# Written-out engine orders for the banded attention pairs, an earlier second norm and three sums on another engine, in a two-layer encoder trunk

## The chip, the cores and the metric

The kernel runs on one core of a Trainium2 chip. The core has five engines with their own instruction queues: TensorE (PE: matrix products and transposes through it), VectorE (DVE), ScalarE (ACT), GpSimd (POOL) and SyncE (SP), which issues the loads and stores. Each queue is worked off in its own order, and the engines wait for one another through semaphores. The metric is the device time of one launch in microseconds, as the median over several runs.

## The reference

The trunk has two layers on 1024 tokens of width 1024, all in fp32. Per layer: a modulated RMSNorm and one input projection, three groups of attention heads side by side, a group-wise RMSNorm, one output projection with a gated residual, then a second modulated RMSNorm and a SwiGLU feed-forward block (hidden width 2816).

```python
h = rms_norm(x, g_attn[l]) * (1 + sc_a) + sh_a
qa, ka, va, qb, kb, vb, qc, kc, vc = split_cols(h @ w_in[l], IN_SPLITS)
ya = neighborhood_attention(...)     # A, 4 heads: 8x16 window on a 16x64 grid, relative bias
yb = sliding_window_attention(...)   # B, 6 heads: |i-j| <= 128, T5 bias, a sink logit
yc = axial_attention(...)            # C, 6 heads: dense, rotary
y = concat([rms_norm(ya, ga), rms_norm(yb, gb), rms_norm(yc, gc)])
x = x + gt_a * (y @ w_o[l])
h = rms_norm(x, g_ffn[l]) * (1 + sc_f) + sh_f
gate, up = split_cols(h @ w_gu[l], (FFN_HIDDEN, FFN_HIDDEN))
x = x + gt_f * ((silu(gate) * up) @ w_down[l])
```

A and B are banded: a block of 128 queries sees at most three blocks of 128 keys. In the kernel the tokens of A are sorted by columns of the grid, so that its window has the same three-block band.

## The kernel before, in words

An fp32 product is formed from parts: each operand is split into a rounded part (`hi`, written by ScalarE) and the rest (`lo`, a subtraction, mostly on VectorE), and three products hi·hi, lo·hi, hi·lo are added in PSUM (`mm3`). So every operand costs a copy on ScalarE and a subtraction on VectorE.

The order of instructions on an engine is set by a scheduler, which orders by dependencies and its own estimate. Where the program calls `pin(engines, True)`, each instruction of these engines is chained behind the one before it in program order, so the written order is the engine's order. GpSimd is pinned throughout the attention; TensorE, ScalarE and VectorE are not in the kernel before.

**Attention.** One list `stream` has 64 pairs; a pair is two blocks of 128 queries of one head: pairs 0 to 23 are dense (C), 24 to 39 are A, 40 to 63 are B. The main loop runs over `n` and keeps several pairs in work: the transposes of pair n (`turn`), the products with V of pair n-1 (`pv`), and the scores of a pair further on (`qk`), three ahead for C, five ahead for the bands (`AHEAD`, `AHEAD_B`).

A band pair goes through these steps:

- scores (`sA`, `sB`): two products per block (rounded and low part of the keys), into one tile of `psS` (two buffers, each with a bank for either block).
- bias step: one VectorE instruction per block adds the bias `z`, writes `pr` and takes the row's extreme (CUSTOM_DVE_ANT in the trace), with an accumulator read.
- exponential: one ScalarE instruction per block with its sum, and an accumulator read.
- division: one reciprocal on VectorE, then two GpSimd multiplications (`pr<-pr,rs`).
- transposes (`T`): four of the inner blocks and one or two of the edge blocks, in tiles of `psT` (three buffers); ScalarE writes the rounded part (`pt<-T` CAST), VectorE the low part (`pt<-T`), and an `edge` copy goes to VectorE in even and ScalarE in odd pairs.
- products with V (`pv`), rounded and low part, into `psV`, which has a single bank shared by two neighbouring pairs; the result has its two halves on different partitions.
- `combine`, in odd pairs: ScalarE copies one half (`cmb<-pv`), VectorE adds both into `y`, and the bank is free again.

A head has four pairs; the first and the last see one edge block, the inner two see both. Beside this run the group norms: squares (`gsq`, `gss`) on ScalarE, sums on GpSimd, statistics on TensorE (`ps_st`) and a short chain of small VectorE steps (`isq`, `rstd`), the transposes `ps_r` with their copies `rb`, and the multiplications `y<-y,rb` on GpSimd. Near the end the first products of the output projection (`ps_o`) and the splits of `w_o` are mixed in.

**Gate/up.** The feed-forward products use a seven-product scheme on 2x2 blocks (`PRODUCTS`); quarter numbers `q` alternate gate (even) and up (odd). The first two products of the first seven quarters (`EARLY`) need only the first half of the tokens and run while the norm of the second half is still being made: `rstd_rows` yields once after the statistics and once with the row of reciprocal roots spread over the partitions (`ps_r`, by four transposes). Then `t2_part`, `t3_part` and `t4_part` make the operands t1, t2, t3, t4 and 22 on VectorE and ScalarE (`h_norm` is the VectorE step that reads `ps_r`). After that the other five products of quarter 0, then of quarter 1, and so on follow; `sg` and `u` hold their sums. Weight operands (`wpt`, from `ws` and `wr`) are made ahead by VectorE, ScalarE and, from the tenth on, GpSimd in turns.

Of the kernel before, what the change touches and what calls it, by code (L numbers as in the profile page):

```python
# [10 lines left out]
F32 = mybir.dt.float32  # L11
# [74 lines left out]
def trunk(ctx: ExitStack, tc, A, C, out):  # L86
# [732 lines left out]
    for l in range(2):  # L819
# [421 lines left out]
        class Pair:  # L1241
# [38 lines left out]
            def combine(self):  # L1280

                r0 = (self.row % 2) * 64
                o0 = 64 - r0
                half = self.p // 2
                t = atp.tile([P, H], F32, name="cmb", tag="cmb", bufs=1)
                act.copy(t[r0 : r0 + 64], self.pvt[o0 : o0 + 64])
                to = y[r0 : r0 + 64, self.row // 2, :]
                a, b = self.pvt[r0 : r0 + 64], t[r0 : r0 + 64]
# [26 lines left out]
        class PairC(Pair):  # L1315
# [21 lines left out]
            def pv(self, part):  # L1337
                self.products(
                    [
                        (kb * 4 + i, slice(0, 256), [t[:, i, :] for t in self.pt[kb]])  # L1340
                        for kb in range(2)
                        for i in range(4)
                    ],
                    part,
                )

# [37 lines left out]
        class Band(Pair):  # L1384
# [10 lines left out]
            def qk(self, c):  # L1395
                rs, p, sk = self.rs, self.p, self.sk
                if c == 0:
                    self.s = psS.tile([P, 2, 512], F32, name=self.name, tag="S")
                s, pr = self.s, self.pr
                j = 2 * p + c  # L1400
                a, b = self.spans[c]
                for i in range(2):
                    pe.matmul(
                        s[:, c, a:b], self.q[:, j * P : (j + 1) * P],
                        self.k[i][:, (j - 1) * P + a : (j - 1) * P + b],
                        start=(i == 0), stop=(i == 1),
                    )
                sv, pw, z = s[:, c, a:b], pr[:, c, a:b], self.bias(j, a, b)
                if z.ndim > 2:
                    sv, pw = (t.rearrange("p (b k) -> p b k", k=P) for t in (sv, pw))  # L1410
                dve.tensor_tensor_reduce(
                    out=pw, in0=sv, in1=z, scale=1.0, scalar=BIG if sk is None else sk,
                    op0=ALU.add, op1=ALU.min, accum_out=rs[:, c : c + 1],
                )
                e = pr[:, c, a : b + (sk is not None)]
                act.activation(
                    e, e, AF.Exp, bias=rs[:, c : c + 1], scale=-1.0,
                    accum_out=rs[:, 2 + c : 3 + c],
                )
                self.finish(pr[:, c, a:b])  # L1420

            def turn(self, c):
                pr = self.pr
                T = t_tile()
                if c == 0:
                    self.pt = [pt_tile() for _ in range(2)]
                    for b in range(2):
                        for i in range(2):
                            pe.transpose(
                                T[:, 2 * b + i, :], pr[:, b, (1 - b + i) * P : (2 - b + i) * P],  # L1430
                                ident,
                            )
                    hv, lv = (
                        t[:, 0:2, :].rearrange("p i (c q) -> p c i q", c=2) for t in self.pt
                    )
                    split_pt(T.rearrange("p (c i) q -> p c i q", c=2), hv, lv)
                    return
                e = self.e = atp.tile([P, 2, P], F32, name="edge", tag="edge", bufs=3)
                n = 0
                for left, here in ((True, self.left), (False, self.right)):  # L1440
                    if here:
                        src = pr[:, 0, 0:P] if left else pr[:, 1, 2 * P : 3 * P]
                        pe.transpose(T[:, n, :], src, ident)
                        n += 1
                if self.p % 2:
                    act.copy(e[:, 0:n], T[:, 0:n])
                else:
                    dve.tensor_copy(e[:, 0:n], T[:, 0:n])

            def pv(self, part):  # L1450
# [8 lines left out]
                self.products(movs, part)  # L1459
# [121 lines left out]
        AHEAD, AHEAD_B = 3, 5  # L1581
        pin((pool,), True)
        made, done = 0, len(first_pairs)
        for n in range(-AHEAD - 1, N + 1):
            ahead = AHEAD if n + AHEAD < 24 else AHEAD_B
            begin = range(done, min(n + ahead + 1, N))
            for i in range(2):
                if 0 <= n < N:
                    pairs[n].turn(i)
                while unfinished:  # L1590
                    unfinished.pop(0)()
                if 0 <= n - 1 < N:
                    pairs[n - 1].pv(i)
                for m in begin:
                    if m < made:
                        pairs[m].qk(i)
            done = max(done, min(begin.stop, made))
            while made < min(N, n + ahead + 2):
# [27 lines left out]
            m = n - 1  # L1626
            for end, (chunks, width) in norms.items():
                if begins[end] <= m <= end and (m - begins[end]) % 8 == 7:
# [22 lines left out]
        pin((pool,), False)  # L1651
# [195 lines left out]
        def gu_product(q, p, a):  # L1847
# [131 lines left out]
        for q in range(EARLY):  # L1979
            for i in range(2):  # L1980
                a = [w[:, 4 * i : 4 * i + 4] for w in early[q]]
                gu_product(q, PRODUCTS[i], a)
            if q + 4 < EARLY:
# [5 lines left out]
            if q == 1:  # L1989
                rows = next(norm)  # L1990
# [357 lines left out]
```

## Time and profile before

| | |
|---|---|
| runs, median (lowest to highest) | 2423.01 us (2418.51 to 2429.48), 3 runs |
| profiled execution | 2422.97 us, span 2421.1 us, mean granted clock 0.994 |
| TensorE busy | 2350.5 us, 97% of the span |
| VectorE, ScalarE, GpSimd busy | 1766.8, 1194.3, 753.4 us |
| bands, layer 0 and layer 1 | first add into `y` at 394.0 and 1574.8 us |
| start of gate/up in layer 0 | first product 583.4 us, remaining products of quarter 0 from 622.9 us |

A line of a group of instructions reads: line, engine, operation, output<-inputs, shape, count, then busy time and mean duration, then the idle time before it and what ended it. All engines' instructions are recorded in one helper, so their line is always L49; the names of the tiles tell them apart. A line of a stretch reads: window, its length, then for TensorE's products, TensorE's weight loads, VectorE, ScalarE and GpSimd the busy time with the count, then the granted clock, the DMA share and GB/s. A line in order of time reads: start, duration (of several in a row together), engine, operation, output<-inputs, shape, count, and in brackets the idle time before it with what ended it. Products overlap in the pipeline, so their durations are longer than the distance of their starts.

### The profile page before, as it was taken

Reading aid. Unit: us, or ns where it says so; the run is one execution under the profiler, and the core shown is the slowest. Engines: PE = TensorE matmul, PEld = TensorE weight load, DVE = VectorE, ACT = ScalarE, POOL = GpSimd, SP = SyncE. Lnnn points to the kernel's source line nnn. Section 1 sums busy time; section 2 is a strip of 40 time slices with the busy share of each in tenths; the row PEclk is TensorE's granted clock in tenths of the full one; section 3 lists DMA queues with packets and bytes.
Section 4 is the critical chain, followed back from the end, with each engine's and each line's share of the span. In section 5 each row is a group of like instructions: output and inputs, shape, how many; then the busy total and the mean of one; then the engine's idle time right before and its main releaser. Section 6 shows DMA issues by size and latency. Waiting matters only on the chain.

```text
span 2421.1 us, 33439 instructions
## 1 busy us (share of the span) xinstructions
PE 2350.5 (97%) x11733; PEld 1955.2 (81%) x11733; DVE 1766.8 (73%) x2782; ACT 1194.3 (49%) x2250; POOL 753.4 (31%) x725
## 2 busy tenths in 40 slices
PE   8999999999999999999999999999999999999998
PEld 5778798888787887888787879987878888888886
DVE  5756898976958888586677579988787545447865
ACT  3421788954543333344543148897454333334443
POOL 1530345610344344300036114464005444430001
PEclk9999999999999999999999999999999999999999
DMA  8478215154245454586434851142524332329643
GB/s 263 149 237 274 62 27 145 47 193 138 87 145 178 157 189 147 176 268 195 148 93 120 283 178 27 45 140 70 194 93 153 125 100 96 114 92 304 209 129 109
DMA packets 305335, 356.95 MB, mean 147 GB/s; under 512 B 51964, under 2 KB 221788, under 8 KB 305168
## 3 DMA queue, kind: packets, MB, share of 16 engines
q1 hardware_dynamic: 283296, 342.07, 44.4%
q10 hardware_dynamic: 21504, 12.59, 2.0%
q8 instruction: 92, 1.51, 0.2%
q14 instruction: 75, 0.61, 0.1%
q0 software_dynamic: 368, 0.17, 0.0%
HBM read 269.79 MB, written 88.63 MB: 148 GB/s over the span
## 4 chain that ended last, share of the span: by engine, by line
PE 48%; DVE 4%; issue 4%; DMA 2%; ACT 2%; POOL 2%; ACTq 0%; SPq 0%; POOLq 0%; DVEq 0%
PE ps_w L49 21%; PE ps_d L49 14%; PE ps_o L49 3%; PE pv L49 2%; PE T L49 2%; PE ps_v L49 2%; PE sC L49 2%; DMA qkd<-qko 1%; ACT pr L49 1%; PE ps_c L49 1%; POOL ct L49 1%; PE ps_ab L49 0%; DVE acc L49 0%; DMA graw<-gpd 0%; POOL pr L49 0%
## 5 line engine op out<-in xcount | busy, mean ns | idle before, releaser
L49 PE MATMUL ps_d<-wpt 128*128 128x512 f32 x1848 | 424.3, 390 | 2.4 <-ACT wpt L49 2.1
L49 PEld LDWEIGHTS ps_d<-wpt 128*128 128x128 f32 x1848 | 345.5, 188 | 76.4 <-issue 3.0
L49 POOL TENSOR_SCALAR pr<-pr,rs 128x1024 f32<-128x1024 f32 (+2 forms) x248 | 187.0, 768 | 227.8 <-DVE rs L49 212.8
L49 POOL TENSOR_TENSOR sg<-sg,u 128x512 f32<-128x512 f32 x86 | 125.5, 1461 | 354.5 <-ACT sg L49 117.9
L49 PE MATMUL pv<-pt,vs 128*128 128x256 f32 x1088 | 181.4, 297 | 7.3 <-ACT pt L49 2.7
L49 ACT CAST wpt<-w 128x512 fp32r<-128x512 f32 x154 | 95.7, 621 | 185.8 <-PE ps_d L49 168.0
L49 DVE TENSOR_TENSOR pt<-T,pt 128x512 fp32r<-128x512 f32 x272 | 178.5, 682 | 8.5 <-ACT pt L49 7.1
L49 PE MATMUL T<-identr,pr 128*128 128x128 f32 x1176 | 175.6, 273 | 2.6 <-ACT edge L49 0.8
L49 ACT CAST pt<-T 128x512 fp32r<-128x512 f32 x272 | 153.1, 586 | 40.5 <-PE T L49 38.1
L49 ACT COPY u<-ps_w 128x512 f32<-128x512 f32 x128 | 75.1, 586 | 192.1 <-PE ps_w L49 192.0
L49 DVE TENSOR_TENSOR wpt<-w,wpt 128x512 fp32r<-128x512 f32 x154 | 108.9, 707 | 82.1 <-ACT wpt L49 82.1
L49 POOL TENSOR_TENSOR wpt<-ws,wpt 128x512 fp32r<-128x512 f32 x80 | 111.6, 1395 | 180.8 <-ACT wpt L49 133.9
L49 PEld LDWEIGHTS pv<-pt,vs 128*128 128x128 f32 x1088 | 143.9, 189 | 21.1 <-DVE y L49 11.1
L49 PEld LDWEIGHTS T<-identr,pr 128*128 128x128 f32 x1176 | 139.9, 140 | 19.7 <-ACT edge L49 2.2
L49 DVE SCALAR_TENSOR_TENSOR acc<-wmt,condT,acc 128x512 f32<-128x512 f32 (+1 forms) x98 | 119.2, 1225 | 47.8 <-DMA wmt<-in_w_mod_dram 47.2
L49 ACT CAST wpt<-ws 128x512 fp32r<-128x512 f32 x176 | 107.8, 622 | 61.4 <-issue 26.6
L49 DVE TENSOR_TENSOR wpt<-ws,wpt 128x512 fp32r<-128x512 f32 x96 | 81.6, 861 | 60.3 <-ACT wpt L49 60.2
L49 DVE TENSOR_TENSOR wpt<-graw,wpt 128x512 fp32r<-128x512 f32 x154 | 110.0, 715 | 19.0 <-ACT wpt L49 19.0
L49 DVE TENSOR_REDUCE rs<-sC 128x1 f32<-128x1024 f32 x88 | 107.3, 1221 | 16.4 <-PE sC L49 12.4
L49 DVE TENSOR_TENSOR ws<-wr 128x512 f32<-128x512 f32 x88 | 80.0, 911 | 51.3 <-POOL wpt L49 48.1
L49 ACT CAST wpt<-graw 128x512 fp32r<-128x512 f32 x154 | 95.0, 617 | 43.3 <-DMA graw<-gpd 37.9
L49 PE MATMUL ps_w<-h22h,wpt 128*128 128x512 f32 x352 | 111.2, 397 | 4.6 <-ACT sg L49 3.6
(298 smaller groups left out, 5964.4 us busy)
## 6 DMA issues: line engine op xcount, KB each, us to landing
wr<-in_w_gu_dram SPq DMA_DIRECT2D x92, 512.0 KB, 4.1
gpd<-sg SPq DMA_DIRECT2D x154, 256.0 KB, 4.4
graw<-gpd SPq DMA_DIRECT2D x76, 512.0 KB, 3.6
w<-in_w_down_dram SPq DMA_DIRECT2D x110, 256.0 KB, 5.4
wmt<-in_w_mod_dram SPq DMA_DIRECT2D x48, 512.0 KB, 6.4
qk<-qkd SPq DMA_DIRECT2D x44, 512.0 KB, 6.8
wst<-in_w_o_dram SPq DMA_DIRECT2D x32, 512.0 KB, 3.7
wmt<-in_w_mod_dram SPq DMA_DIRECT2D x64, 256.0 KB, 3.8
```

Of the source, the lines that this page charges most:

```text
L49: ins = op(*args, **kwargs)
```

## The change

1. **Bands.** `Band.qk` is split into `scores` (four score products of both blocks, then both bias steps), `exps` and `divide`; `turn` does all transposes at once and leaves the low part for later (`low`); `pv` does both parts. `combine` is split: `fold` copies one half to `cmb`, `combine` adds. For n from 24 on, TensorE, ScalarE and VectorE are pinned, and the loop body writes out a step: low part of pair n-1, add of n-3, scores and bias steps of n+4, exponentials of n+3, transposes of n, products of n-2 with their fold, division of n+2. `AHEAD_B` goes from 5 to 4. The work in `later` (the group norms) is left unpinned; the splits of `w_o` and of `y` and the first `ps_o` products in the loop fall under the pin. The norms count pairs by n-3 in the bands.
2. **Gate/up, second norm.** `next(norm)`, which issues the four `ps_r` transposes, moves from behind both products of quarter 1 to behind its first.
3. **Gate/up, three sums.** For q of 0 and 1 the sum `t22 + x` and for q of 1 the multiplication of `e` go from GpSimd to VectorE.
4. An unused tile (`pad(ct, 48)`) moves addresses.

```diff
+            pad(ct, 48)
...
-                if part and self.p % 2:
-                    self.combine()
...
+            def fold(self):
+                if self.p % 2 == 0:
+                    return
...
+                self.t = atp.tile([P, H], F32, name="cmb", tag="cmb", bufs=1)
+                act.copy(self.t[r0 : r0 + 64], self.pvt[o0 : o0 + 64])
...
-        AHEAD, AHEAD_B = 3, 5
+        AHEAD, AHEAD_B, NC = 3, 4, 24
...
+            if n == NC:
+                pin((pe, act, dve), True)
...
+                if NC <= n - 1 < N:
+                    pairs[n - 1].low()
+                if NC <= n - 3:
+                    pairs[n - 3].combine()
+                fresh = [pairs[m] for m in begin if m < made]
+                for b in fresh:
+                    b.scores()
+                for b in scored:
+                    b.exps()
+                if n < N:
+                    pairs[n].turn()
+                if NC <= n - 2 < N:
+                    pairs[n - 2].pv()
+                    pairs[n - 2].fold()
+                elif n == NC:
+                    for i in range(2):
+                        pairs[n - 1].pv(i)
+                for b in worked:
+                    b.divide()
+                scored, worked = fresh, scored
...
+            pin((pe, act, dve), False)
             for what in later.pop(n, []):
                 what()
+            pin((pe, act, dve), n >= NC)
...
-                pool.tensor_tensor(out=t22, in0=t22, in1=t["x"], op=ALU.add)
+                (pool if q > 1 else dve).tensor_tensor(out=t22, in0=t22, in1=t["x"], op=ALU.add)
...
                 gu_product(q, PRODUCTS[i], a)
+                if q == 1 and i == 0:
+                    rows = next(norm)
...
-            if q == 1:
-                rows = next(norm)
...
-                    pool.tensor_tensor(out=e, in0=e, in1=quads[q]["11"], op=ALU.mult)
+                    (pool if q > 1 else dve).tensor_tensor(
+                        out=e, in0=e, in1=quads[q]["11"], op=ALU.mult
+                    )
```

The new `scores`, beside which `exps` and `divide` only take the ScalarE and the division steps of the old `qk`:

```python
def scores(self):
    s, pr = psS.tile([P, 2, 512], F32, name=self.name, tag="S"), self.pr
    for c, (a, b) in enumerate(self.spans):      # both blocks' products first
        for i in range(2):
            pe.matmul(s[:, c, a:b], ...)
    for c, (a, b) in enumerate(self.spans):      # then both bias steps
        dve.tensor_tensor_reduce(out=pw, in0=sv, in1=z, ..., accum_out=rs[:, c : c + 1])
```

More of the change, by code (lines that the diff above doesn't have):

```diff
@@ L1345, in pv @@
                 )
+                if part:
+                    self.fold()
+                    self.combine()
         def load_q(dst, oc, j):
@@ L1422, in turn @@
[L1422 to L1448, printed above, removed]
@@ new lines, in exps, with divide, turn @@
+            def exps(self):
+                for c, (a, b) in enumerate(self.spans):
+                    e = self.pr[:, c, a : b + (self.sk is not None)]
+                    act.activation(
+                        e, e, AF.Exp, bias=self.rs[:, c : c + 1], scale=-1.0,
+                        accum_out=self.rs[:, 2 + c : 3 + c],
+                    )
+            def divide(self):
+                divide([self.pr[:, c, a:b] for c, (a, b) in enumerate(self.spans)], self.rs)
+            def turn(self):
+                pr = self.pr
+                T, self.pt = t_tile(), [pt_tile() for _ in range(2)]
+                for b in range(2):
+                    for i in range(2):
+                        pe.transpose(
+                            T[:, 2 * b + i, :], pr[:, b, (1 - b + i) * P : (2 - b + i) * P], ident
+                        )
+                edges = [pr[:, 0, 0:P]] * self.left + [pr[:, 1, 2 * P : 3 * P]] * self.right
+                E = t_tile()
+                for i, src in enumerate(edges):
+                    pe.transpose(E[:, i, :], src, ident)
+                hi, lo = (
+                    t[:, 0:2, :].rearrange("p i (c q) -> p c i q", c=2) for t in self.pt
+                )
+                T = T.rearrange("p (c i) q -> p c i q", c=2)
+                act.copy(hi, T)
+                e = self.e = atp.tile([P, 2, P], F32, name="edge", tag="edge", bufs=3)
+                (act.copy if self.p % 2 else dve.tensor_copy)(
+                    e[:, 0 : len(edges)], E[:, 0 : len(edges)]
+                )
+                self.low = lambda: sub(lo, T, f32(hi))
@@ L1451, in pv @@
+            def pv(self):
                 k0, e = 2 * self.p, self.e
@@ L1458, in pv @@
                     movs.append((k0 + 2, slice(P, 2 * P), [e[:, int(self.left)]]))
-                self.products(movs, part)
+                for part in range(2):
+                    self.products(movs, part)
         class PairA(Band):
```

84 lines of the change are left out of this document (42 added, 42 removed).

## The prediction

> **What bounds the kernel now.** I read the page's first part, then the stretches (busy time of each engine in a window), then the order of time on single engines. TensorE is the bound on paper, and in most stretches it has no gap.
>
> ```profile
> PE 2350.5 (97%) x11733; PEld 1955.2 (81%) x11733; DVE 1766.8 (73%) x2782; ACT 1194.3 (49%) x2250; POOL 753.4 (31%) x725
> ...
> 386.00:490.00 104.00, 99.32 (x717) 87.56 (x716) 94.08 (x297) 94.92 (x252) 66.20 (x118) 1.00 0.36 101
> ...
> 632.00:637.00 5.00, 2.24 (x8) 1.32 (x7) 5.00 (x5) 2.28 (x5) 3.15 (x3) 0.91 0.45 148
> 637.00:642.00 5.00, 5.00 (x18) 3.95 (x18) 4.08 (x6) 2.48 (x5) 1.27 (x1) 0.75 0.62 209
> ```
>
> The change touches two places in each of the two layers. The first is the bands (386 to 490 us in layer 0). There VectorE is busy 94.08 of 104 us and ScalarE 94.92, so three engines are near full at once, and nobody can gain more than ScalarE's idle 104 - 94.92 = 9.1 us a layer from a better order alone. The second is the start of gate/up (622 to 642 us), where TensorE really stands still and its clock then falls to 0.91 and 0.75. The profiled execution took 2422.97 us (span 2421.1), the median of the runs is 2423.01; I count from 2422.97.
>
> **The bands: how fast they go before.** Two neighbouring pairs share one pv bank and end in one add into y, so the starts of these adds are the beat.
>
> ```profile
> L49 DVE TENSOR_TENSOR y<-pv,cmb x20: 661/689/695, 394.0 to 492.5; 64x512 f32<-64x512 f32 x20
> ...
> 420.79 0.68 DVE L49 TENSOR_TENSOR y<-pv,cmb 64x512 f32<-64x512 f32 x1
> ...
> 439.25 0.66 DVE L49 TENSOR_TENSOR y<-pv,cmb 64x512 f32<-64x512 f32 x1
> ...
> 468.33 0.68 DVE L49 TENSOR_TENSOR y<-pv,cmb 64x512 f32<-64x512 f32 x1
> ...
> 492.47 0.69 DVE L49 TENSOR_TENSOR y<-pv,cmb 64x512 f32<-64x512 f32 x1
> ```
>
> Twenty adds from 394.0 to 492.5 are 19 beats of 98.5 / 19 = 5.18 us. In 420.79 to 439.25 (4 beats) and 468.33 to 492.47 (5 beats), where no statistics of a norm stand, it is (18.46 + 24.14) / 9 = 4.73 us. So the norms and the start cost 98.5 - 19 x 4.73 = 8.6 us a layer.
>
> **The bands after.** No arithmetic is added or taken away. Each step n is now written out: on TensorE the four score products of pair n+4, the transposes of n, the products with V of n-2; on ScalarE the two exponentials of n+3, the rounded copy of n, an edge copy in odd n, the cmb copy of n-2; on VectorE the low part of n-1, the add into y of n-3, the two bias steps of n+4, an edge copy in even n, the reciprocal for n+2. So I add up TensorE's own issue time from starts of neighbouring groups, and then ask what it has to wait for.
>
> ```profile
> 381.06 0.87 PE L49 MATMUL sA<-qk 128*128 128x384 f32 x4
> 381.76 1.04 PE L49 MATMUL T<-identr,pr 128*128 128x128 f32 x8
> ...
> 421.53 0.74 PE L49 MATMUL pv<-pt,vs 128*128 128x256 f32 x4
> 422.10 0.61 PE L49 MATMUL pv<-edge,vs 128*128 128x128 f32 x4
> 422.47 0.37 PE L49 MATMUL pv<-pt,vs 128*128 128x256 f32 x1
> ...
> 424.69 0.82 PE L49 MATMUL T<-identr,pr 128*128 128x128 f32 x6
> 425.26 0.59 PE L49 MATMUL sB<-qk 128*128 128x384 f32 x2
> ...
> 475.65 0.39 PE L49 MATMUL pv<-edge,vs 128*128 128x128 f32 x2
> ...
> 472.32 0.58 ACT L49 COPY cmb<-pv 64x512 f32<-64x512 f32 x1
> ...
> 476.13 0.58 ACT L49 COPY cmb<-pv 64x512 f32<-64x512 f32 x1 [0.46 <-PE pv L49]
> ...
> 472.93 0.69 DVE L49 TENSOR_TENSOR y<-pv,cmb 64x512 f32<-64x512 f32 x1 [0.55 <-ACT cmb L49]
> ...
> 473.68 0.74 PE L49 MATMUL pv<-pt,vs 128*128 128x256 f32 x4 [0.57 <-DVE y L49]
> ```
>
> An inner pair costs TensorE 0.70 (four scores, 381.06 to 381.76) + 0.57 (six transposes) + 0.57 (four products) + 0.37 (two edges) = 2.21 us. An outer pair has five transposes and one edge: 0.70 + 0.48 + 0.57 + 0.19 = 1.94. Four pairs of a head: 8.3 us.
>
> The wait is a ring through three in-order engines. There is one pv bank, so an even pair's products wait for the add, which waits for the cmb copy, which waits for the odd pair's products. TensorE has issued the last edge about 0.19 after 475.65, so near 475.84; the copy starts 476.13, 0.29 later; from its start to the next products (472.32 to 473.68) are 1.36. The ring takes 1.65 us. Between the two, TensorE has the scores and transposes of the next pair, 0.70 + 0.48 or 0.57 = 1.18 to 1.27. It waits about 0.4 us, twice a head. Once a head the edge transposes wait for VectorE's low part of the pair before, which frees their buffer (three T buffers, two used by a pair): I take 0.3, between 0 and a step of the size of the add, 0.69. A head: 8.3 + 0.8 + 0.3 = 9.4 us, a beat of 4.70.
>
> The cover holds elsewhere. Scores lead by four steps instead of five. A division on GpSimd is issued two steps (4.7 us) ahead of the transposes that read it, against these rows:
>
> ```profile
> L49 POOL TENSOR_SCALAR pr<-pr,rs 128x384 f32<-128x384 f32 x56 | 33.0, 598 | 21.4 <-DVE rs L49 19.3 <-ACT pt L49 1.4 <-PE sA L49 0.6
> L49 POOL TENSOR_TENSOR y<-y,rb 128x512 f32<-128x512 f32 x10 | 12.9, 1287 | 0.0
> L49 POOL COPY pr<-sinkc 128x2 f32<-128x2 f32 x24 | 4.5, 189 | 0.0
> ...
> wst<-in_w_o_dram SPq DMA_DIRECT2D x32, 512.0 KB, 3.7
> ```
>
> Two divisions, one norm multiplication and a sink copy are 1.20 + 1.29 + 0.19 = 2.7 us, against a step of 2.35: in the at most six steps in a row that carry a multiplication GpSimd falls behind by 0.35 each, 2.1 in all, and the lead left over is 4.7 - 2.7 = 2.0. So 0, at worst 0.7 twice a layer. The norms' statistics, the rb copies and the squares stay unpinned and keep their 8.6 us; their bounds are half of it (hidden in the ring's waits) and half more (the ring holds them up). At the end the splits of w_o stand pinned on ScalarE and VectorE ahead of two low parts, behind a load that starts when the split before frees its buffer: 3.7 us, and about as much again for the splits and the low part. TensorE has two pairs' transposes and products (3 us) and 18 w_o products at 0.23 us (12 in 592.48 to 595.20, below) to run meanwhile. I count 0, between -1 and 2 us. The changed mixing at the first band pairs I count the same, with the same bounds. SP's queue keeps its order, and the pad issues nothing.
>
> Bands: 19 x (4.73 - 4.70) = 0.6 us a layer. Bounds: 9.1 gained (ScalarE never idle, above), and as much lost if ring and norms go against it (0.48 us a beat).
>
> **Gate/up.** The second norm's rows (ps_r) move ahead of one product.
>
> ```profile
> 592.48 0.39 PE L49 MATMUL ps_w<-h21h,whi 128*128 128x512 f32 x1
> ...
> 595.20 0.60 PE L49 MATMUL ps_r<-identr,rstd 128*128 128x128 f32 x4
> ...
> 595.47 0.69 DVE L49 TENSOR_TENSOR u<-u,ps_w 128x512 f32<-128x512 f32 x1 [4.29 <-PE ps_w L49]
> ...
> 629.35 0.73 PE L49 MATMUL ps_w<-ht3h,wpt 128*128 128x512 f32 x2 [0.81 <-ACT sg L49]
> 633.32 0.73 PE L49 MATMUL ps_w<-ht4h,wpt 128*128 128x512 f32 x2 [0.96 <-ACT u L49]
> 636.54 1.22 PE L49 MATMUL ps_w<-h22h,wpt 128*128 128x512 f32 x2 [1.80 <-ACT sg L49]
> 640.76 0.39 PE L49 MATMUL ps_w<-ht4l,wpt 128*128 128x512 f32 x1
> ...
> 635.90 0.59 ACT L49 COPY sg<-ps_w 128x512 f32<-128x512 f32 x1 [2.64 <-DVE ht4l L49]
> ...
> 631.79 1.77 DVE L49 TENSOR_TENSOR ht4l<-xb,ht4h 128x512 fp32r<-128x512 f32 x1
> 633.49 1.78 DVE L49 SCALAR_TENSOR_TENSOR h22l<-xb,mod,h22h 128x512 fp32r<-128x512 f32 x1
> 635.19 0.68 DVE L49 TENSOR_TENSOR ht4l<-xb,ht4h 128x512 fp32r<-128x512 f32 x1
> 637.22 1.60 DVE L49 TENSOR_TENSOR ht4l<-xb,ht4h 128x512 fp32r<-128x512 f32 x1
> ...
> 631.32 3.40 POOL L49 TENSOR_TENSOR sg<-sg,u 128x512 f32<-128x512 f32 x2 [114.15 <-DMA wr<-in_w_gu_dram]
> 636.57 1.71 POOL L49 TENSOR_TENSOR sg<-sg,u 128x512 f32<-128x512 f32 x1 [1.85 <-ACT sg L49]
> ```
>
> VectorE idles 4.29 us until 595.47 and is then full to 637. The transposes of ps_r would start at 592.48 in place of 595.20, so 12 matmuls or 2.72 us sooner, and VectorE can take up h_norm about 0.7 later, near 593.2: its queue starts 2.3 us sooner. Then the sums: beside GpSimd's sums three VectorE steps take 1.77, 1.78 and 1.60 in place of 0.68, which is 3.1 us lost. Two of the three moved sums stand here; they add 2 x 0.6 on VectorE, and one GpSimd sum stays, which still costs about 1.1. Net 3.1 - 1.1 - 1.2 = 0.8 us. VectorE is 2.3 + 0.8 = 3.1 us sooner at the last ht4l. That is what ScalarE's sg copy (2.64 us idle for ht4l) and through it TensorE's 1.80 us wait for, and the 0.81 hangs on the ht3h copies of the same chain. Of 0.81 + 0.96 + 1.80 = 3.57 us, the 0.96 (t4 after its own u copy) stays. After the gaps 12 matmuls (636.54 to 640.76) take 4.22 in place of 2.72, as the granted clock of 0.75 says: 1.5 us more, which goes with them. TensorE could win 0.81 + 1.80 + 1.5 = 4.1, but next it needs the weights of quarter 1, which come behind the same VectorE queue, now shorter by 3.1. I take 3.2 us a layer, bounds 1.0 (the weights' queue eats it) and 5.1 (all of it). The third sum, of quarter 1, adds 0.6 on VectorE where TensorE has no gap: 0, at worst 0.6.
>
> The clock: these rows show it low behind gaps of at most 1.80 us. [...]
>
> **Sum.** 2422.97 - 2 x 0.6 - 2 x 3.2 = 2415.4, so 2415 us, or 0.3% faster.
>
> **Rivals.** (1) The written order keeps ScalarE and VectorE full: against it the ring above, for it the 9 to 10 us that both idle. At two thirds of 9.1, 6 us a layer, it gives 2422.97 - 12 - 6.4 = 2405; at all of it 2398. (2) Slower: the ring. The cmb copy now stands in a fixed place behind exponentials, and each tenth that it is late goes into every beat, since there is one pv bank. For it: in the rows above both the add and the products already wait for it (0.55, 0.57). Against: the copy is written behind the products it needs, with spare time before it. The sign turns where the mean beat passes 5.18 + 6.4 / 38 = 5.35; at 5.6 us a layer loses 19 x 0.42 = 8, and the whole takes 2422.97 + 16 - 6.4 = 2433. (3) Gate/up does not gain: VectorE stays the bound, the wait moves from the sg copy to the weights of quarter 1. At 1.0 a layer: 2420.
>
> **How the numbers follow.** Forecast 0.42, with its own range 2410 to 2420; rival 1 0.28; rival 2 0.18; rival 3 0.12. Half a per cent is 12 us, about what a measurement of this kernel can tell from no change: below 2410.9 is faster, above 2435.1 slower. Faster: rival 1 nearly whole and a fifth of the forecast, 0.36. Slower: two thirds of rival 2, 0.13, since its ring may grow further than 5.6. Same: 0.51. The range of 2399 to 2433 leaves out the ends of rivals 1 and 2.
>
> **What would show it.** Right: adds into y with a mean beat near 5.15, TensorE's products waiting for y about twenty times a layer at 0.4 us, no waits of the scores for rs; in gate/up h_norm on VectorE near 593, no ht4l or h22l over 1.2 us but one, the 1.80 us gap under 0.5, the clock not under 0.9. Wrong: a beat under 4.9 or over 5.35, a gap in front of ht2 of quarter 1 of over 1.5 us, or a new wait of the w_o products at the end of the bands.

## The result, and the profile after

The changed kernel takes 2437.07 us (median of 8 runs, 2432.3 to 2440.57) against 2423.17 us (8 runs, 2418.3 to 2429.48) on the same chip. The ratio is 1.0058, with a 95% interval of 1.0043 to 1.0073. So it is slower by 14 us, where 8 us less (2415) was forecast, and it lies above the range of 2399 to 2433. Its profiled execution, the longest of the eight, has a span of 2438.8 us and a mean granted clock of 0.989, against 2421.1 and 0.994.

The first part of its page shows no more work than before (TensorE was 2350.5 us busy, VectorE 1766.8):

```profile
PE 2347.7 (96%) x11733; PEld 1963.8 (81%) x11733; DVE 1761.2 (72%) x2788; ACT 1193.9 (49%) x2250; POOL 741.6 (30%) x719
```

The adds into `y` show where the time went. First, in order of time, two rows of the kernel before that the prediction did not have, the first and the last of the twenty adds of layer 0:

```profile
399.05 0.68 DVE L49 TENSOR_TENSOR y<-pv,cmb 64x512 f32<-64x512 f32 x1
...
499.16 0.69 DVE L49 TENSOR_TENSOR y<-pv,cmb 64x512 f32<-64x512 f32 x1 [0.47 <-ACT cmb L49]
```

Then the first, 5th, 10th, 14th and 20th of the changed kernel:

```profile
397.73 0.68 DVE L49 TENSOR_TENSOR y<-pv,cmb 64x512 f32<-64x512 f32 x1
...
418.96 0.68 DVE L49 TENSOR_TENSOR y<-pv,cmb 64x512 f32<-64x512 f32 x1 [0.53 <-ACT cmb L49]
...
443.09 0.67 DVE L49 TENSOR_TENSOR y<-pv,cmb 64x512 f32<-64x512 f32 x1
...
466.48 0.68 DVE L49 TENSOR_TENSOR y<-pv,cmb 64x512 f32<-64x512 f32 x1 [0.29 <-ACT cmb L49]
...
510.08 0.69 DVE L49 TENSOR_TENSOR y<-pv,cmb 64x512 f32<-64x512 f32 x1
```

Up to the 14th add (468.33 before) both kernels need about the same: 468.33 - 399.05 = 69.3 us before, 466.48 - 397.73 = 68.8 after. From the 14th to the 20th it is 499.16 - 468.33 = 30.8 us before and 43.6 after. The last six beats lose 12.8 us in layer 0, and the same stretch of layer 1 loses the same (30.76 to 43.55). The span of the profiled executions grew by 17.7 us (2421.1 to 2438.8), so in them all the rest together is 17.7 - 12.8 - 12.8 = -7.9 us, shorter than before.

The stretches of these six beats, before and after:

```profile
468.33:499.16 30.83, 28.29 (x187) 23.97 (x187) 28.33 (x59) 25.17 (x57) 14.63 (x26) 1.00 0.19 62
```

```profile
466.48:510.08 43.60, 33.07 (x193) 29.83 (x194) 29.46 (x63) 27.28 (x60) 15.84 (x27) 0.88 0.19 57
```

No engine is full in the second. TensorE stands still for 43.60 - 33.07 = 10.5 us instead of 2.5, and its busy time is 4.8 us longer, at a granted clock of 0.88. The waits of TensorE in 466 to 510 us (total, times, longest) name one releaser above all:

```profile
PE pv L49 <- DVE y L49: 9.6, 3, 5.4
PE pv L49 <- ACT whi L49: 1.4, 1, 1.4
```

The longest of the three, 5.39 us, in order of time on ScalarE, VectorE and TensorE:

```profile
483.91 0.58 ACT L49 COPY cmb<-pv 64x512 f32<-64x512 f32 x1
484.40 0.72 ACT L49 ACTIVATE qk<-y,vecs 128x512 fp32r<-128x512 f32 x1
485.02 1.03 ACT L49 CAST whi<-wst 128x1024 fp32r<-128x1024 f32 x1
...
487.18 0.59 ACT L49 CAST pt<-T 128x512 fp32r<-128x512 f32 x1
```

```profile
485.15 0.75 DVE L49 SCALAR_TENSOR_TENSOR qk<-y,vecs,qk 128x512 fp32r<-128x512 f32 x1 [1.16 <-ACT qk L49]
486.08 2.02 DVE L49 TENSOR_TENSOR wlo<-wst,whi 128x1024 fp32r<-128x1024 f32 x1 [0.18 <-ACT whi L49]
488.03 0.68 DVE L49 TENSOR_TENSOR pt<-T,pt 128x512 fp32r<-128x512 f32 x1
488.63 0.67 DVE L49 TENSOR_TENSOR y<-pv,cmb 64x512 f32<-64x512 f32 x1
```

```profile
489.45 1.19 PE L49 MATMUL pv<-pt,vs 128*128 128x256 f32 x4 [5.39 <-DVE y L49]
```

This is the end of step 59, where a split of `y` (the tile `qk<-y`) and a split of `w_o` (`whi`, `wlo`) are written behind the pair's instructions. The copy `cmb` is done at 484.5, and the add that needs it could follow. But VectorE's queue now holds the two splits (waiting for ScalarE's half of them), then the low part, and only then the add, at 488.63. The add frees the single pv bank, so TensorE waits until 489.45, and the transposes of the next pair stand behind that (491.29). The rounded copy at 492.39 is late in turn (4.62 us of ScalarE idle for `T`), and so is the next `whi` behind it.

### The profile page after: what moved, and what is told of

Read it like the earlier page. It is cut to its first block, busy times and chain, and to the rows that moved or that the text cites. A ratio compares the mean times of both kernels' runs of the same rounds, so it can differ in the third digit from the quotient of the medians.

```text
span 2438.8 us, 33440 instructions
## 1 busy us (share of the span) xinstructions
PE 2347.7 (96%) x11733; PEld 1963.8 (81%) x11733; DVE 1761.2 (72%) x2788; ACT 1193.9 (49%) x2250; POOL 741.6 (30%) x719
## 5 line engine op out<-in xcount | busy, mean ns | idle before, releaser
L49 POOL TENSOR_TENSOR sg<-sg,u 128x512 f32<-128x512 f32 x82 | 116.0, 1416 | 353.1 <-ACT sg L49 228.0
L49 PE MATMUL T<-identr,pr 128*128 128x128 f32 x1176 | 164.2, 276 | 0.7 <-DVE pt L49 0.4
L49 DVE TENSOR_TENSOR wlo<-wst,whi 128x1024 fp32r<-128x1024 f32 x66 | 83.1, 1261 | 50.9 <-ACT whi L49 48.0
L49 DVE TENSOR_REDUCE rs<-sC 128x1 f32<-128x1024 f32 x88 | 107.3, 1221 | 15.2 <-PE sC L49 10.5
```

The source lines that it names most:

```text
L49: ins = op(*args, **kwargs)
```

## The experiments

All ratios are to the kernel before on the same chip; its medians lay between 2422.4 and 2423.4 us.

| kernel | median us | ratio | 95% interval |
|---|---|---|---|
| changed | 2437.1 | 1.0058 | 1.0043 to 1.0073 |
| gate/up edits alone | 2413.1 | 0.9966 | 0.9953 to 0.9979 |
| bands alone | 2447.6 | 1.0101 | 1.0084 to 1.0118 |
| other work free | 2416.9 | 0.9977 | 0.9966 to 0.9987 |
| unpinned from step 54 | 2417.7 | 0.9987 | 0.9978 to 0.9996 |
| splits of y free | 2430.0 | 1.0034 | 1.0020 to 1.0048 |
| splits of w_o free | 2428.2 | 1.0028 | 1.0017 to 1.0038 |
| written order for A only | 2417.4 | 0.9980 | 0.9966 to 0.9993 |
| copy off the ring | 2415.0 | 0.9971 | 0.9961 to 0.9981 |
| no copy | 2413.5 | 0.9955 | 0.9941 to 0.9970 |
| lead of five | 2417.6 | 0.9977 | 0.9965 to 0.9989 |
| earlier norm alone | 2416.9 | 0.9975 | 0.9963 to 0.9987 |
| three sums alone | 2418.6 | 0.9978 | 0.9967 to 0.9990 |
| sink copy first | 2412.6 | 0.9958 | 0.9943 to 0.9972 |
| sink copy first, lead of five | 2414.3 | 0.9963 | 0.9952 to 0.9975 |

**The two halves of the change, each alone.** The kernel before with parts 2 and 3 of the change, by their lines of its diff:

> The kernel before with the gate/up edits alone (earlier second norm, three sums on VectorE), the bands untouched. In the trace of the changed kernel the lag against before shrinks from 9.38 to 5.48 us across the start of gate/up in layer 0 and from 19.76 to 15.03 in layer 1, so if the two edits act alone as they do there: 2423.2 - 3.9 - 4.7 = 2414.6 us. If the gain there was borrowed from the late bands (work that waited anyway), under 1 us a layer: 2421 to 2423. In layer 0 the changed kernel gives 2.8 us back about 150 us later, where two gaps of 1.17 and 1.47 us are followed by a granted clock of 0.57; if that belongs to the earlier gate/up, 2417.4.

The changed kernel with these lines taken back:

> The changed kernel without the gate/up edits: bands and mixing alone. If the two parts of the change are independent, before + 10.6 (layer 0) + 10.5 (layer 1) from the lag at the end of the bands: 2423.2 + 21.1 = 2444 us. If the late bands fed the gain in gate/up, nearer to the changed kernel: 2437.

Measured: -9.9 us and +24.5 us (1.5 us under and 3.6 over what was expected), which add up to +14.6; the whole change is +13.9. As far as the runs can tell, the two are independent. Gate/up alone is a gain of 0.34%, the bands alone a loss of 1.0%. The unused tile of the change goes with the bands here and was not run by itself.

**Freeing the other work of the loop.** The theory was that the pinned splits break the rhythm; the rival that the written order with one pv bank is slow in itself.

```diff
-            if n == NC:
+            if n >= NC:
                 pin((pe, act, dve), True)
...
             for what in later.pop(n, []):
                 what()
-            pin((pe, act, dve), n >= NC)
```

> The changed kernel, with the other work of the loop (splits of y and w_o, w_o rows, first output products, last norm sums) left free like the group norms; the written steps of the pairs stay pinned to the end. Theory T (the pinned splits of the last steps stand ahead of low part and add in the queues of ScalarE and VectorE, and the single pv bank carries each delay on to TensorE): the last six beats, 37 to 44 us long in the changed kernel, come back to about 4.7 to 5.2 each, 8 to 10 us a layer, 2417 to 2421 us. Rival R (the written order itself with the one pv bank is what is slow, the splits only stand beside it): under 2 us a layer, 2433 to 2437.

Measured 2416.9, at the edge of the first theory's range and 20 us under the changed kernel. The same six beats and their waits:

```profile
465.49:498.60 33.11, 29.43 (x196) 26.20 (x197) 27.48 (x61) 26.08 (x58) 18.72 (x28) 1.00 0.21 65
```

```profile
PE pv L49 <- DVE y L49: 2.3, 3, 1.3
```

43.60 - 33.11 = 10.5 us came back: 6.8 of TensorE's idle time (10.5 to 3.7) and 3.6 of its busy time, with the clock at 1.00 again. The rival falls for nearly all of the loss: 2.3 of the 12.8 us are left (33.1 against 30.8).

**Everything unpinned from step 54**, the pairs' steps too:

```diff
+            if n == 54:
+                pin((pe, act, dve), False)
...
-            pin((pe, act, dve), n >= NC)
+            pin((pe, act, dve), NC <= n < 54)
```

> The changed kernel with TensorE, ScalarE and VectorE given back to the scheduler from step 54 on, for the pair steps as well as for the splits; steps 24 to 53 stay written out. Theory T: as with only the splits free, 2417 to 2421. Rival R (the written pair steps are slow by themselves): gains in the last ten steps alone and more than freeing only the splits, by 2 us a layer or more. A third way: the scheduler, with the low part and the add at the head of each step, places them worse than its old order did, 2424 to 2432.

2417.7 us, and 32.4 us for the six beats of either layer, 0.7 and 0.5 less than from freeing the other work alone; from the first add to the last it is 102.4 us in layer 0 in both. So the written steps of the pairs are not what is slow there.

**Which split.** Only the splits of `y` (steps 55 and 59) unpinned, then only those of `w_o` (59 and 61); both edits in one diff:

```diff
             if n in (55, 59):
...
+                pin((pe, act, dve), False)
                 y_split(...)
+                pin((pe, act, dve), True)
...
             if n in (59, 61):
+                pin((pe, act, dve), False)
                 w01.append(split_tile(...))
+                pin((pe, act, dve), True)
```

> The changed kernel with only the two splits of y (steps 55 and 59) left free. In the changed kernel the adds of steps 56 and 58 come 2.2 and 1.3 us later than with all the other work free, that of step 60 2.9 and that of step 62 3.9 us. If each pinned piece costs what stands behind it, the first 3.5 us a layer belong to the split of y at step 55, and up to 2.9 to the one at step 59: 2437 - 7 to 2437 - 13 = 2424 to 2430 us. If the splits of y only stood in the shadow of the splits of w_o: 2435 to 2437.

> The changed kernel with only the two splits of w_o (steps 59 and 61) left free. By the beats: 3.9 us a layer for the one at step 61 and up to 2.9 for the one at step 59, so 2437 - 8 to 2437 - 14 = 2423 to 2429 us. If any one pinned piece is enough to break the rhythm, under 2 us a layer: 2433 to 2437.

Measured 2430.0 and 2428.2. The six beats are 38.3 and 39.2 us in layer 0 (38.6 and 39.7 in layer 1), against 43.6: 5.3 and 4.4 us in layer 0, together 9.7 of the 10.5. In layer 1 they are 5.0 and 3.9, together 8.8 of 10.7; what is left over, up to 1.9 us, belongs to the rest of the freed work or to the splits together. Each piece costs its share, and neither stands in the shadow of the other.

**Is the written order any good without them?** On the kernel with free other work, for the pairs of A alone (steps 24 to 41):

```diff
-            if n >= NC:
+            if NC <= n < 42:
                 pin((pe, act, dve), True)
```

> The changed kernel with the other work free and the written order only for steps 24 to 41 (the pairs of A). With the other work free the last six beats are still 33.1 us long against 30.8 before, the first ones 0.5 to 1.2 us ahead. If the written order only loses at the end, this keeps the lead and drops the loss: 2409 to 2413 us, level with the gate/up edits alone (2413) or up to 4 us better. If the scheduler needs to recover behind the written part: 2413 to 2418.

2417.4, no better than with the order written to the end, as the rival had it. The first 13 beats take 68.1 us against 69.3 before the change, and the last six 34.7 against 30.8, which uses up the lead.

**What sets the clean beat.** The prediction named the ring through the pv bank. From the 6th to the 10th add, four beats without statistics of a norm, the kernel with free other work takes 422.28 to 441.53, 4.81 us each. First the copy is taken out of the ring, at the same load on ScalarE and VectorE (the diffs here and below are shortened):

```diff
 def fold(self):
...
-    act.copy(self.t[r0 : r0 + 64], self.pvt[o0 : o0 + 64])
+    act.copy(t[r0 : r0 + 64], old[o0 : o0 + 64])      # old: 512 columns of vs
 def combine(self):
...
+    self.t = old
```

> The changed kernel with free other work, and the copy of the pv half taken out of the ring: ScalarE makes a copy of the same size from values in SBUF, and VectorE adds other values that stand ready (so y of the bands is wrong). ScalarE and VectorE have the same work, but the even pair's products wait only for the add. In the beats without norm work (five from the fifth to the tenth add, 4.82 us each with the copy in the ring) the ring theory of the prediction expects the half microsecond in front of the products to go: 4.3 to 4.45. If ScalarE (22.9 of 24.1 us busy there) and VectorE (22.1) are the bound, the beat stays at 4.7 to 4.85. Whole time: ring theory 19 x 0.4 x 2 = 15 us less than with the copy, 2402; full engines 2414 to 2418.

Then it is left out altogether (the `act.copy` line goes):

> As the kernel with the copy off the ring, but with no copy at all: ScalarE loses one instruction of 0.58 us a beat, VectorE adds ready values as there (so y of the bands is wrong). With the copy off the ring the clean beats stayed at 4.81 us, so the ring through the copy is not what sets them. If ScalarE is (22.9 to 23.1 of 24.1 us busy over five clean beats), the beat falls by up to 0.5, until VectorE with 22.1 of 24.1 us, 4.43 a beat, sets it: 4.4 to 4.5, and 19 x 0.35 x 2 = 13 us in all, 2402 to 2404. If neither: 4.75 to 4.85 and 2413 to 2417.

The stretches of these four beats, each kernel by its own adds: free other work, copy off the ring, no copy.

```profile
422.28:441.53 19.25, 17.38 (x133) 16.19 (x132) 17.77 (x58) 18.14 (x51) 14.72 (x30) 1.00 0.25 88
```

```profile
421.34:440.57 19.23, 16.88 (x128) 15.95 (x129) 17.76 (x57) 18.24 (x51) 14.70 (x30) 1.00 0.26 89
```

```profile
423.78:443.03 19.25, 16.88 (x128) 15.93 (x129) 17.77 (x58) 15.90 (x47) 14.72 (x30) 1.00 0.26 90
```

19.25, 19.23, 19.25: the beat does not move, though ScalarE's work falls from 18.14 to 15.90 us in the last. (With the beat from the fifth add on, as the expectations count, it is 4.94 and 4.95 us in the last two against 4.82.) As what sets these beats, both theories, the ring and ScalarE's load, fall. In the second of these kernels TensorE still waits for the add (417 to 442):

```profile
PE pv L49 <- DVE y L49: 2.5, 4, 0.9
```

So the wait in front of the products only filled time that something else sets. Outside the clean beats the copy may have a share: from the first add to the last these two kernels take 100.5 to 101.4 us, and 102.4 and 103.2 in the two layers with the copy in the ring.

What was left in the trace with free other work were VectorE's bias steps that wait for GpSimd, again in 417 to 442. The line of these waits comes first, then a step in order of time on VectorE and GpSimd:

```profile
DVE pr L49 <- POOL pr L49: 1.5, 5, 0.4
```

```profile
434.23 0.16 DVE L49 RECIPROCAL rs<-rs 128x2 f32<-128x2 f32 x1
...
435.76 0.48 DVE L49 CUSTOM_DVE_ANT_0 pr<-sB,bz,sinkc 128x256 f32<-128x256 f32 x1 [0.26 <-POOL pr L49]
436.17 0.09 DVE L49 DVE_READ_ACCUMULATOR2_ANT rs<- 128x1 f32 x1
436.17 0.16 DVE L49 RECIPROCAL rs<-rs 128x2 f32<-128x2 f32 x1
```

```profile
434.55 1.05 POOL L49 TENSOR_SCALAR pr<-pr,rs 128x256 f32<-128x256 f32 x2 [1.74 <-DVE rs L49]
435.54 0.19 POOL L49 COPY pr<-sinkc 128x2 f32<-128x2 f32 x1
```

Reciprocal at 434.23, two divisions from 434.55, behind them the sink copy of a later pair at 435.54, which the second bias step at 435.76 needs, and the next reciprocal at 436.17: a ring through GpSimd's queue. The test is to put that small copy ahead of the divisions, in GpSimd's order alone:

```diff
+                create(n, ahead)          # makes the next pair, with its sink copy
                 for b in worked:
                     b.divide()
```

> The changed kernel with free other work; GpSimd's copy of the sink column for the next pair stands ahead of the two divisions of its step instead of behind them, everything else in the same order. Theory G: the clean beats are set by a ring through GpSimd's queue (VectorE's reciprocal, two divisions, sink copy, VectorE's second bias step, reciprocal), since five bias steps in 24 us wait 1.5 us for that copy while neither the pv ring nor ScalarE's load moved the beat. The waits of bias steps for GpSimd go and the clean beats fall from 4.81 by 0.2 to 0.39 (VectorE's idle share there, 24.10 - 22.14 = 1.96 us over five beats): 4.4 to 4.6, over the twelve beats of B 2.4 to 4.7 us a layer, 2408 to 2412 us. Rival: VectorE's own order is the limit and the wait only fills time that would pass anyway: 4.75 to 4.85, 2414 to 2418.

The same four beats, and then VectorE's and TensorE's waits in 417 to 442:

```profile
425.45:444.07 18.62, 17.49 (x134) 16.34 (x133) 17.54 (x56) 17.82 (x51) 15.26 (x31) 1.00 0.27 95
```

```profile
DVE y L49 <- ACT cmb L49: 1.2, 4, 0.5
...
PE pv L49 <- DVE y L49: 1.6, 3, 0.6
```

4.66 us a beat, and the waits for GpSimd are gone: the ring through its queue was a limit, though the gain of 0.15 is under the 0.2 to 0.39 expected, and the whole at 2412.6 stands just outside the 2408 to 2412. The add now waits for `cmb` (1.2 us against 0.6), so the ring of the prediction may come next; no run here shows it. From the first add to the last the bands still take 101.3 and 101.5 us, more than the 100.1 and 99.9 before the change.

**The lead.** Five in place of four, with free other work, and with the sink copy first:

```diff
-        AHEAD, AHEAD_B, NC = 3, 4, 24
+        AHEAD, AHEAD_B, NC = 3, 5, 24
```

> The changed kernel with free other work and a lead of five band pairs, as before the change, in place of four. With the lead of four and the other work free, the last six beats of the bands are 33.1 us long in layer 0 against 30.8 before. If the shorter lead is what leaves them longer: 31 us, 2 x 2.3 us less, 2412 to 2413. If not: 2416 to 2418. The clean beats stay at 4.8 in either case.

> As the kernel with the sink copy first, with a lead of five in place of four. A lead of five took the last six beats from 33.1 to 31.4 us a layer in the profile. If theory G holds and the two add up: 2405 to 2409 us, faster than the gate/up edits alone (2413). With the lead of five the sink copy waits for the transposes of the same step; if that puts GpSimd behind, the clean beats come out above those of the lead of four and the whole at 2414 to 2420.

With the lead of five the last six beats take 31.4 us in both layers (33.1 and 32.9 with four), and with both edits 30.9 and 30.8, as before the change. From the first add to the last it is then 99.2 us against 100.1. The clean beats, though, come out longer: 4.90 against 4.81, where 4.8 was expected, and 4.76 against 4.66, as the second half of the last expectation has it. The whole shows no gain: 2417.6 and 2414.3, no faster than with the lead of four. In the profiles other parts, which the edit does not touch, differ by up to 5 us from kernel to kernel (the first add stands at 396.2 in one and 401.1 in the other); and the interval of each whole is about 3 us to either side; a gain of 2 us a layer is hard to tell from that. Of the versions that leave nothing out, the fastest are the gate/up edits alone (2413.1) and the written order with free other work and the sink copy first (2412.6), level with one another.

**Gate/up, its two edits apart.** On the kernel before, the moved `next(norm)` alone, and then the three sums alone, again by the lines of the change's diff:

> The kernel before with the earlier second norm alone and its two moved sums of quarter 0 and 1 (t22 + x, e) left on GpSimd. The prediction gave the norm 2.3 of 3.1 us a layer. By that share of what both edits brought (2423 to 2413): 2423 - 7 = 2416 us. If VectorE steps stretched by GpSimd's sums (1.77, 1.78, 1.60 us in place of 0.68) are the larger part: 2419 to 2421.

> The kernel before with the three sums on VectorE alone, the second norm where it was. The prediction gave the sums a net 0.8 us a layer: 2421 us. If the stretched steps on VectorE are the larger part: 2416 to 2418. If the sums only add their 0.6 us each to a full VectorE: 2424.

Measured -6.5 and -4.9 us; both in one kernel were -9.9. The norm alone came out as its share had it (2416.9 for 2416), the sums alone at 2418.6, between the two figures expected. The stretches that answer to 632 to 637 and 637 to 642 of the prediction, with the norm alone and then with the sums alone:

```profile
632.00:637.00 5.00, 2.68 (x11) 1.59 (x10) 4.91 (x5) 2.47 (x5) 3.75 (x3) 1.00 0.46 146
637.00:642.00 5.00, 5.00 (x23) 3.84 (x22) 4.96 (x8) 3.10 (x6) 0.63 (x1) 1.00 0.77 242
```

```profile
632.00:637.00 5.00, 3.36 (x14) 2.15 (x13) 5.00 (x8) 2.87 (x6) 1.27 (x1) 1.00 0.62 196
637.00:642.00 5.00, 4.88 (x21) 3.49 (x20) 5.00 (x10) 3.16 (x6) 0.00 (x0) 1.00 0.64 197
```

With either edit alone the gaps are shorter (the longest for `sg` is 1.6 us with the norm and 0.8 with the sums, against 1.80 before), and the clock stays at 1.00, where before it was 0.91 and 0.75. That part of the gain is had by either one.

## Why the prediction was wrong

**End of the bands: here it failed.** "At the end the splits of w_o stand pinned on ScalarE and VectorE ahead of two low parts ... I count 0, between -1 and 2 us." Freeing the loop's other work gave back 10.5 us in layer 0 and 10.7 in layer 1; the splits freed one kind at a time gave 9.7 and 8.8. Three things were missed. The splits of `y` stand under the same pin and were not priced; they are half of it (5.3 and 5.0 us). The price was taken from the load that the split waits for and compared with TensorE's work at hand (transposes, products, 18 `w_o` products). But the add stands in the same queue behind the splits, and with one pv bank TensorE cannot take up the next pair's products until the add is done, however much work there would be later in its order. And behind the gaps the clock fell to 0.88 over the six beats, where 3.6 of the 10.5 us were longer busy time.

**The count of the beats** was off by one: the adds at 394.0 and 1574.8, named as the first of the bands, belong to the last dense pair (the bands' first are at 399.05 and 1579.87), and the window ended before the twentieth at 499.16. The mean beat before is 100.11 / 19 = 5.27, not 5.18, and its last beat alone is 6.7 us long. That would have pointed at the end of the bands as a tight place already.

**The clean beat.** Forecast 4.70, 0.03 less than the beat taken for before; measured (443.09 - 418.96) / 5 = 4.83, against 4.77 before from the same adds. The size was near, but the sign and the reason were not right: taking the copy out of the pv ring and taking 2.2 us off ScalarE in four beats left the beat where it was, and GpSimd's queue ("0, at worst 0.7 twice a layer") held 0.15 us of every one of these beats, by way of the sink copy behind the divisions. That its waits for the add were there as forecast (five in 417 to 442, 0.5 us each) did not make them the limit. Up to the 14th add the bands gained 0.5 us in layer 0 and 0.4 in layer 1, where the forecast had 0.6 over all beats; but in the kernel with the bands alone, whose bands are the same, that stretch takes 69.95 us in either layer, 0.7 and 0.8 more than before, so a gain is not shown.

**Rival 2** had the right sign, and its turning point held: the mean beat is 112.35 / 19 = 5.91, over 5.35. Its mechanism, a `cmb` copy late behind exponentials in every beat, did not: in the 5.39 us wait above the copy was on time, and the add stood behind the splits. Rival 1 fell with the clean beat (no version of the written order gained more than 1 us a layer from the first add to the last), rival 3 with the next point. The first band pairs were counted 0. Their first add stands 1.3 us sooner here, but in the kernels whose bands are untouched it stands anywhere from 396.8 to 400.4, so that shows nothing; from the last add of the dense pairs to it, it is 5.1 us before and 6.6 us after.

**Gate/up was right in mechanism.** `h_norm` starts at 602.50, which is 593.4 when the 9.1 us are taken off by which the first product of gate/up is late (583.4 to 592.5), and the forecast named 593; beside the one GpSimd sum left there a single VectorE step takes 1.78 us. Stretches of the changed kernel that answer to the prediction's, with the gaps of its products:

```profile
636.00:641.00 5.00, 4.57 (x21) 3.45 (x19) 5.00 (x9) 4.32 (x7) 0.18 (x1) 1.00 0.15 53
641.00:646.00 5.00, 4.70 (x21) 3.87 (x22) 5.00 (x8) 1.99 (x4) 1.16 (x1) 1.00 0.89 291
```

```profile
641.30 0.73 PE L49 MATMUL ps_w<-ht4h,wpt 128*128 128x512 f32 x2 [0.73 <-ACT u L49]
...
647.63 0.50 PE L49 MATMUL ps_w<-ht2h,wpt 128*128 128x512 f32 x1 [0.57 <-ACT wpt L49]
```

The gaps of 0.81 and 1.80 us are gone, the one of 0.96 stays at 0.73, the weights of quarter 1 take 0.57, and the clock is 1.00. The first products of t2 in quarters 0 and 1 before, and the one in quarter 0 after:

```profile
622.87 0.39 PE L49 MATMUL ps_w<-ht2h,wpt 128*128 128x512 f32 x1
...
642.36 0.39 PE L49 MATMUL ps_w<-ht2h,wpt 128*128 128x512 f32 x1
```

```profile
632.25 0.61 PE L49 MATMUL ps_w<-ht2h,wpt 128*128 128x512 f32 x2
```

The first product of t2 in quarter 0 starts 9.38 us later than before (622.87 to 632.25), the first one of quarter 1 only 5.27 us later (642.36 to 647.63): 4.1 us gained in layer 0, and 4.3 in layer 1 by the same rows (19.76 to 15.50), where 3.2 was forecast. The sum for both layers, 6.4, was 8.4 in these profiles and 9.9 us alone on the chip, with an interval of 5.1 to 11.4 that holds both. Of the 4.1 us in layer 0 the gaps gave 2.3 (3.57 to 1.30) and the slow stretch the other 1.8, against 1.5 in the forecast. The term that was too large is what was taken off for the weights of quarter 1: 0.9 us, where their wait is 0.57. The norm and the sums cannot be held against their terms one by one: between the same rows the norm alone gains 3.0 us in layer 0 and 3.1 in layer 1, the sums alone 2.5 and 2.6, which is 1.3 and 1.5 more than both together, since either by itself ends the slow stretch.

**The clock.** The sum went by the rows, in which the 1.5 us of slow clock come behind gaps of at most 1.80 us, and took it that they go with the gaps. The rows held: with gaps of at most 0.7 us in either layer the slow stretch is gone. In the kernel before the clock falls there in both layers (0.75 in 637 to 642, 0.66 in 1817 to 1822). In the changed kernel it stays at 1.00 in both, and so it does in ten others that have one of the gate/up edits or both. How short a gap has to be for that, no run here shows.

## What to carry to other kernels

When an order is written out by hand, price everything that falls under it, above all the rare pieces between the steps: a 2 us instruction in a queue costs what stands behind it there, not what it takes (here `wlo`, 2.02 us, stood ahead of an add for which TensorE waited 5.39). Where one buffer ties two engines together (here a pv bank that is free only after an add), no other work may stand in that queue ahead of the instruction that frees it. And a wait that the profile shows is a limit only if the beat moves when it is taken away: a copy in the ring and a part of ScalarE's load were taken away here and the beat stayed, and what moved it, by 0.15 us, was the place of a 0.19 us copy.

## What the runs showed of the hardware

The same two gaps can cost nothing or 2.6 us. About 200 us into gate/up of layer 0, TensorE waits twice for the modulation of the next layer (`ps_mod`). First the kernel with the gate/up edits alone, its two gaps and four stretches of one us; then the kernel unpinned from step 54, its two gaps and the stretches around them:

```profile
779.98 0.51 PE L49 MATMUL ps_mod<-acch,onesr 128*128 128x512 f32 x1 [1.17 <-DVE acch L49]
781.96 0.80 PE L49 MATMUL ps_mod<-accl,onesr 128*128 128x512 f32 x1 [1.47 <-DVE accl L49]
```

```profile
781.00:782.00 1.00, 0.04 (x1) 0.04 (x1) 1.00 (x2) 0.00 (x0) 0.36 (x1) 0.64 0.00 0
782.00:783.00 1.00, 1.00 (x3) 0.82 (x4) 1.00 (x2) 0.00 (x0) 0.00 (x0) 0.50 0.09 10
...
787.00:788.00 1.00, 1.00 (x4) 0.81 (x3) 0.01 (x1) 0.04 (x1) 0.00 (x0) 0.50 0.75 260
788.00:789.00 1.00, 1.00 (x5) 0.77 (x5) 1.00 (x2) 0.87 (x2) 0.00 (x0) 0.95 0.10 37
```

```profile
784.07 0.50 PE L49 MATMUL ps_mod<-acch,onesr 128*128 128x512 f32 x1 [1.17 <-DVE acch L49]
786.05 0.50 PE L49 MATMUL ps_mod<-accl,onesr 128*128 128x512 f32 x1 [1.48 <-DVE accl L49]
```

```profile
784.00:788.00 4.00, 2.46 (x9) 1.79 (x10) 3.96 (x7) 0.10 (x1) 1.27 (x1) 1.00 0.20 47
788.00:792.00 4.00, 4.00 (x19) 3.30 (x18) 3.67 (x7) 1.26 (x2) 0.00 (x0) 1.00 0.96 336
```

In the first the clock is 0.50 from about 781.3 (0.64 is the mean of that us) to 788.1, 6.8 us; in the second it stays at 1.00. Of 14 kernels (all but "bands alone" and "other work free" of the table), the clock fell at these gaps in nine, for 6.8 or 6.9 us in four (the changed one among them) and for about 3.4 us in five; in the other five, the kernel before among them, it stayed at 1.00. Where the stretches are 5 us long, these lengths are estimates, which take the clock of the fall as 0.50: with the earlier norm alone it is 0.73 in 785 to 790 and 0.93 in 790 to 795, and (5 x 0.27 + 5 x 0.07) / 0.50 = 3.4 us. From the first of these products to the next product of t2 it is 4.91 us in the kernel before (786.03 to 790.94) and 5.06 in the one with no copy (781.03 to 786.09), both without the fall, and 7.68 in the changed one (791.35 to 799.03), where it lasts 6.8 us. In layer 0 of the changed kernel the distance to the kernel before grew there from 5.48 to 8.32 us, which gave back more than half of what gate/up had gained in that layer (2.8 of 4.1 us). The two gaps together are 2.64 or 2.65 us in five kernels, two with the fall (the changed one and the gate/up edits alone) and three without (before, unpinned from step 54, no copy), so a single profile cannot show an edit to be at fault for it. The two with the fall have gaps of 1.17 and 1.47 us and a product of 0.5 us between them; unpinned from step 54, gaps of 1.17 and 1.48 us with the same product between them brought none. What decides it, no trace here shows.
